# A hybrid SSD and GLA layer: the first block's gates one per step, and GpSimd's operand sums of the second part divided around the last head's power

## The chip, the cores and the metric

The kernel runs on one core of a Trainium2 chip. The metric is the time of one execution in microseconds (us), as the device measures it. The median of three runs of the kernel before is 2242.24 us.

A core has a tensor engine (TensorE, PE: matmuls from SBUF into PSUM banks), a vector engine (VectorE, DVE), a scalar engine (ScalarE, ACT: activation functions and copies), GpSimd (POOL) and a synchronisation engine (SyncE, SP), which here only issues transfers. Each engine works its own queue in order, and an instruction can wait for a semaphore that another engine or a DMA sets.

## The reference

One layer with two branches over the same input: `D_MODEL` is 1024, the sequence has 2048 tokens behind 16 learned meta tokens, all in float32. Cut to what matters here:

```python
u = rmsnorm(h, norm_w)
proj = u @ w_in                     # z, xbc, dt, q, k, v, g_gla, a_lr (rank 16), merge_g
xbc = silu(causal_depthwise_conv(xbc, conv_w, conv_b))            # 4 taps
y_ssd = ssd_chunked(xs, dt, a, bm, cm) + d_skip * xs              # 4 groups of 4 heads
y_ssd = group_rmsnorm(y_ssd * silu(z))
log_a = log_sigmoid(a_lr @ gla_gate_w2 + gla_gate_b) / 16         # 4 heads of 128
o = rmsnorm(gla_chunked(q, k, v, log_a))                          # 4 heads, chunks of 64
y_gla = o * silu(g_gla)
merged = sigmoid(merge_g[0]) * (y_ssd @ w_branch[0]) + sigmoid(merge_g[1]) * (y_gla @ w_branch[1])
out = rmsnorm(h + merged @ w_out)[meta:]
```

## The kernel before

**Numbers.** Every large matmul is an fp32 product made of three matmuls: each operand is divided into a high and a low part (`fp32r`), and `accum` (L214 to L216) adds high by high, high by low and low by high in PSUM. "Splitting" an operand means that ACT copies it into the high part and DVE subtracts the high part from the operand to get the low one.

**The first part** works through four blocks of 512 tokens (`nblk`; the first has the 16 meta tokens in addition, `m0`), up to about 1476 us. A block's work is a set of Python generators: the projections (`proj_zm`, `proj_conv`, `proj_z`, `proj_qk`, `proj_v`) one after another, and beside them the scans (`ssd_scan` for each of the four SSD groups, `gla_scan` for each of the four GLA heads) and the decay gates (`gates`). `step()` advances each running generator up to its next `yield`. So a `yield` says how far a generator's instructions come in one step, and what stands between them is a piece of a projection. The order of PE's and SP's queues is the order of the code (`tc.manual_schedule`); DVE, ACT and POOL are put in order by a scheduler that works with times of its own. `tc.issue_after(x)` tells that scheduler to place what follows behind instruction x; it adds no semaphore.

PSUM has eight banks in three pools: `pj` with three (projections, and in the first block the gates), `pt` with three (transposes) and `pc` with two (scans).

**The first block's gates.** `gates` makes the decay of the four heads in pairs. For each head h, PE multiplies with `gla_gate_w2` (L488, two matmuls of 264 columns in the first block, one into a bank of `pj` and one into a bank of `pt`); DVE (L490) and ACT (L491, absolute value) both read each bank. Behind the two heads of a pair ACT takes an exponential and a logarithm over both (L493, L494), and then a `yield` follows. In the first block the running sums of each head (L498 and one scan L500 for each chunk) are put off to the end of a step (`put_off`). At the same time the first block runs the convolution: PE's projection, eviction by ACT into two tiles (L595, L596), three multiply-adds on DVE (L600), tanh on ACT (L603), one more on DVE (L604), and then the first SSD group's scan: per chunk `before` (PE transposes L664, DVE, the decay mask with its square L680) and `after` (PE L689, L690 and L692, DVE).

**The last block's last head.** `gla_scan` ends with a norm: ACT sums squares, `rstd_of` scales on DVE (L258) and takes the power -0.5 on POOL (L259), ACT scales the four chunks (L969), PE transposes them (L976), DVE multiplies (L977) and ACT stores them (L980).

**The second part** does merge gates, branch products and the output product in stages. Each pair of output tiles is made of seven products in place of eight (products 1, 2, 6, 7, 5, 3, 4 in this order, `PS`). A product needs four B tiles (`load_b`, `prep_b`: ACT L1108, DVE L1109) and one A operand (`prep_a`: ACT L1133, DVE L1134), twelve matmuls for each operand. There are two operands n for each product at a time. `load_a` (L1115) loads four raw tiles `ar` of an operand; `sum_a` makes on POOL what the products need of them:

```python
nc.gpsimd.tensor_tensor(s1, a21, a22, op=ALU.add)         # L1124, product 5
nc.gpsimd.tensor_tensor(s2, s1, a11, op=ALU.subtract)     # L1125, product 6
nc.gpsimd.tensor_tensor(a21, a11, a21, op=ALU.subtract)   # L1126, product 7
nc.gpsimd.tensor_tensor(s4, a12, s2, op=ALU.subtract)     # L1127, product 3
```

The three sums go to tiles `as` (a ring of six, used by snapshots of PSUM as well), `a21` stays in place. The table `between` runs the second part's first loads, sums, splits and products (1, 2 and 6 of operands 0 and 1) in between the last steps of the last head; behind it, `at(pos, fn)` files an action for a position in the list of products and `run(i)` runs what is due.

## Time and the profile before

| | before |
|---|---|
| median of three runs | 2242.24 us (2240.61, 2242.24, 2245.01) |
| the profiled execution | 2246.45 us, its span 2244.7 us |
| PE matmul busy | 2211.9 us (99%), 11789 instructions |
| PE weight load busy | 1896.8 us (85%) |
| DVE busy | 1577.0 us (70%) |
| ACT busy | 1187.0 us (53%) |
| POOL busy | 693.9 us (31%) |
| DMA | 517.95 MB, mean 231 GB/s |
| granted PE clock, mean | 0.997 |

The busy times are of the profiled execution. Weight loads run beside matmuls, and the ends of matmuls are modelled, so 99% says that there is hardly a place where PE stands still, and not that it runs at its peak. Rows of a timeline give start and duration in us, engine, line, operation, output and inputs, tile shape, count, and in brackets the wait ahead of the instruction with what ended it. A group's row gives total busy time in us and the mean of one in ns. In the rows by stretch the engines stand in the order PE, weight loads, DVE, ACT, POOL, then the granted clock, the DMA share and GB/s. Names are those of the program without their numbers: `act`, `sq`, `c` and `tok4` are working tiles, `pj`, `pt` and `pc` PSUM banks, `whl` and `ue` the split weights and inputs of the first part, `a` and `b` the split operands of the second, `ar` and `br` their raw tiles.

### The profile page before, as it was taken

Reading aid. Unit: us, or ns where it says so; the run is one execution under the profiler, and the core shown is the slowest. Engines: PE = TensorE matmul, PEld = TensorE weight load, DVE = VectorE, ACT = ScalarE, POOL = GpSimd, SP = SyncE. Lnnn points to the kernel's source line nnn. Section 1 sums busy time; section 2 is a strip of 40 time slices with the busy share of each in tenths; the row PEclk is TensorE's granted clock in tenths of the full one; section 3 lists DMA queues with packets and bytes.
Section 4 is the critical chain, followed back from the end, with each engine's and each line's share of the span. In section 5 each row is a group of like instructions: output and inputs, shape, how many; then the busy total and the mean of one; then the engine's idle time right before and its main releaser. Section 6 shows DMA issues by size and latency. Waiting matters only on the chain.

```text
span 2244.7 us, 34971 instructions
## 1 busy us (share of the span) xinstructions
PE 2211.9 (99%) x11789; PEld 1896.8 (85%) x11789; DVE 1577.0 (70%) x2935; ACT 1187.0 (53%) x2767; POOL 693.9 (31%) x689
## 2 busy tenths in 40 slices
PE   7999999999999999999999999999999999999998
PEld 7999999888888888888988888878888888888887
DVE  5775676677557676567677666674679945789866
ACT  5666655575445456544465544454644545454544
POOL 5444433223212122221212100066233374324341
PEclk9999999999999999999999999999999999999999
DMA  9767875767777667778667664376768866787753
GB/s 313 247 222 234 273 259 202 237 209 240 240 244 260 212 213 237 241 245 272 207 212 233 213 211 160 127 250 198 241 227 289 303 221 217 237 282 245 261 177 121
DMA packets 313699, 517.95 MB, mean 231 GB/s; under 512 B 28080, under 2 KB 162480, under 8 KB 313520
## 3 DMA queue, kind: packets, MB, share of 16 engines
q1 hardware_dynamic: 247008, 419.89, 57.8%
q10 hardware_dynamic: 65872, 93.74, 11.5%
q8 instruction: 92, 1.51, 0.3%
q0 software_dynamic: 640, 2.10, 0.2%
q14 instruction: 87, 0.71, 0.1%
HBM read 368.42 MB, written 147.19 MB: 230 GB/s over the span
## 4 chain that ended last, share of the span: by engine, by line
PE 89%; DVE 4%; DMA 3%; ACT 2%; issue 1%; POOL 1%; SPq 0%; POOLq 0%; ACTq 0%; DVEq 0%
PE pj L214 20%; PE pj L216 20%; PE pj L215 19%; PE pt L215 4%; PE pt L214 4%; PE pt L216 4%; PE pc L689 2%; PE pc L214 2%; PE pc L216 2%; PE pc L215 2%; PE pc L850 2%; PE pc L690 1%; DMA acc<-in_xmt 1%; PE pc L692 1%; PE pc L958 1%
## 5 line engine op out<-in xcount | busy, mean ns | idle before, releaser
L214 PE MATMUL pj<-ue,whl 128*128 128x264 f32 (+1 forms) x672 | 235.3, 350 | 1.9 <-ACT acc L596 1.2
L216 PE MATMUL pj<-ue,whl 128*128 128x264 f32 (+1 forms) x672 | 229.7, 342 | 0.0
L215 PE MATMUL pj<-ue,whl 128*128 128x264 f32 (+1 forms) x672 | 228.8, 340 | 0.0
L214 PE MATMUL pj<-uo,whl 128*128 128x512 f32 x512 | 205.7, 402 | 0.0
L216 PE MATMUL pj<-uo,whl 128*128 128x512 f32 x512 | 200.1, 391 | 0.0
L215 PE MATMUL pj<-uo,whl 128*128 128x512 f32 x512 | 199.5, 390 | 0.0
L214 PE MATMUL pj<-b,a 128*128 128x512 f32 (+1 forms) x484 | 188.9, 391 | 0.7 <-DVE io L1252 0.5
L216 PE MATMUL pj<-b,a 128*128 128x512 f32 (+1 forms) x484 | 188.9, 390 | 0.3 <-DVE a L1134 0.3
L215 PE MATMUL pj<-b,a 128*128 128x512 f32 (+1 forms) x484 | 187.6, 388 | 0.0
L600 DVE SCALAR_TENSOR_TENSOR acc<-cin,hcw,acc 128x512 f32<-128x512 f32 (+1 forms) x192 | 156.7, 816 | 39.7 <-ACT acc L596 38.6
L83 POOL TENSOR_TENSOR wr<-wr 128x256 f32<-128x256 f32 x80 | 66.0, 826 | 371.8 <-DMA wr<-y 158.1
L1124 POOL TENSOR_TENSOR as<-ar,ar 128x512 f32<-128x512 f32 x40 | 62.9, 1572 | 374.7 <-DMA ar<-in_w_br 179.9
L1134 DVE TENSOR_TENSOR a<-ar,a 128x512 fp32r<-128x512 f32 x160 | 130.8, 824 | 65.0 <-ACT a L1133 63.5
L1109 DVE TENSOR_TENSOR b<-br,b 128x512 fp32r<-128x512 f32 x140 | 128.9, 943 | 18.1 <-ACT b L1108 17.8
L214 PEld LDWEIGHTS pj<-ue,whl 128*128 128x128 f32 x672 | 126.2, 188 | 17.7 <-ACT acc L596 1.7
L216 PEld LDWEIGHTS pj<-ue,whl 128*128 128x128 f32 x672 | 126.4, 188 | 14.9
L215 PEld LDWEIGHTS pj<-ue,whl 128*128 128x128 f32 x672 | 126.4, 188 | 14.7
L177 POOL TENSOR_TENSOR whl<-wr,whl 128x512 fp32r<-128x512 f32 (+1 forms) x76 | 96.9, 1282 | 126.2 <-ACT whl L175 94.4
L1168 ACT ACTIVATE sn<-pj 128x512 f32<-128x512 f32 x118 | 70.0, 593 | 123.8 <-PE pj L216 70.8
L1134 DVE TENSOR_TENSOR a<-as,a 128x512 fp32r<-128x512 f32 x120 | 101.6, 848 | 45.2 <-ACT a L1133 42.5
L1133 ACT ACTIVATE a<-ar 128x512 fp32r<-128x512 f32 x160 | 99.0, 624 | 64.7 <-PE pt L216 30.2
L215 PE MATMUL pt<-b,a 128*128 128x512 f32 x320 | 125.6, 392 | 3.9 <-DVE b L1109 3.9
(329 smaller groups left out, 6467.6 us busy)
## 6 DMA issues: line engine op xcount, KB each, us to landing
whl<-k_s SPq DMA_DIRECT2D x96, 512.0 KB, 3.7
whl<-k_g SPq DMA_DIRECT2D x96, 512.0 KB, 4.3
whl<-k_v SPq DMA_DIRECT2D x36, 512.0 KB, 4.0
wr<-in_w_feat SPq DMA_DIRECT2D x64, 256.0 KB, 4.5
k_s<-whl SPq DMA_DIRECT2D x32, 512.0 KB, 3.9
cb<-cumd SPq DMA_DIRECT2D x64, 256.0 KB, 5.1
y<-gg ACTq DMA_DIRECT2D x64, 256.0 KB, 4.2
k_g<-whl SPq DMA_DIRECT2D x32, 512.0 KB, 4.0
```

What stands on the lines that cost most here:

```text
L83: nc.gpsimd.tensor_tensor(o, x, y, op=ALU.subtract)
L177: nc.gpsimd.tensor_tensor(hl[:, 1], raw, hl[:, 0].bitcast(F32), op=ALU.subtract)
L214: nc.tensor.matmul(ps, sh, mh, start=first, stop=False, **kw)
L215: nc.tensor.matmul(ps, sh, ml, start=False, stop=False, **kw)
L216: nc.tensor.matmul(ps, sl, mh, start=False, stop=last, **kw)
L600: convd[:] = [nc.vector.scalar_tensor_tensor(acc, cin[:, k:k + tt], hcw[:, ti, k:k + 1], acc, op0=ALU.mult, op1=ALU.add)]
L689: nc.tensor.matmul(py[:, h * 64:(h + 1) * 64], dm[:, h], xdt[:, h], start=True, stop=True)
L1109: nc.vector.tensor_tensor(t[:, 1], raw, t[:, 0].bitcast(F32), op=ALU.subtract)
L1124: nc.gpsimd.tensor_tensor(s1, a21, a22, op=ALU.add)
L1133: nc.scalar.activation(t[:, 0], src, AF.Copy)
L1134: latest[:] = [nc.vector.tensor_tensor(t[:, 1], src, t[:, 0].bitcast(F32), op=ALU.subtract)]
L1168: nc.scalar.activation(sn, self.ps[n, "a"], AF.Copy)
```

## The change

**Gates.** In the first block `gates` now has a `yield` behind head 2. Head 3's matmuls, its evictions and the exponential and logarithm of the pair come one step later, and so does what the generator does behind them.

**Sums.** `sum_a` stays for later operands. For operands 0 and 1 of the second part it is divided: `sum_first` (s1 and s2) is called in row 2 of `between`, ahead of the last head's power; `sum_second` (the difference in `a21`) and `sum_third` (s4) are filed for positions -0.5 and 0. The last head's `rstd_of` is placed behind the last of the first sums, and the split of product 6 for operands 0 and 1 behind the last of the four scalings (L969), both with `issue_after`.

```diff
 # gates, inside the loop over the heads of a pair
                     evicted[:] = [nc.scalar.activation(g_all[:, h, a:a + n], ps[:, :n], AF.Abs, bias=gb)]
+                if m0 and h == 2:
+                    yield
             ga = g_all[:, h2:h2 + 2, :tt]
...
 # gla_scan, the norm at its end
-        r = rstd_of(ssq, 4, 1.0 / 256)
+        with tc.issue_after(summed[-1].ins) if o.b == nblk - 1 and h == GH - 1 and summed else nullcontext():
+            r = rstd_of(ssq, 4, 1.0 / 256)
         for c in range(NCH):
-            nc.scalar.activation(ot[:, c], ot[:, c], AF.Identity, scale=r[:, c:c + 1])
+            scaled[:] = [nc.scalar.activation(ot[:, c], ot[:, c], AF.Identity, scale=r[:, c:c + 1])]
...
-    early_b = {}
+    early_b, summed, scaled = {}, [], []
...
+        def sum_first(self, n):
+            a11, a21, a22, a12 = self.araws[n]
+            s1, s2 = [mk(rpl, [P, 4, P], F32, "as", bufs=NAS) for _ in range(2)]
+            nc.gpsimd.tensor_tensor(s1, a21, a22, op=ALU.add)
+            summed[:] = [nc.gpsimd.tensor_tensor(s2, s1, a11, op=ALU.subtract)]
+            self.a[n].update({4: a22, 5: s1, 6: s2})
+
+        def sum_second(self, n):
+            a11, a21, a22, a12 = self.araws[n]
+            nc.gpsimd.tensor_tensor(a21, a11, a21, op=ALU.subtract)
+            self.a[n][7] = a21
+
+        def sum_third(self, n, s2):
+            a12 = self.araws.pop(n)[3]
+            s4 = mk(rpl, [P, 4, P], F32, "as", bufs=NAS)
+            nc.gpsimd.tensor_tensor(s4, a12, s2, op=ALU.subtract)
+            self.a[n][3] = s4
...
         def prep_a(self, n, p):
...
-            nc.scalar.activation(t[:, 0], src, AF.Copy)
+            with tc.issue_after(scaled[-1].ins) if n < 2 and p == 6 and self is stages[0] else nullcontext():
+                nc.scalar.activation(t[:, 0], src, AF.Copy)
...
+    second = {}
+
+    def first_sums(n):
+        st.sum_first(n)
+        second[n] = st.a[n][6]
+
+    for n in range(2):
+        at(-0.5, lambda n=n: st.sum_second(n))
+        at(0, lambda n=n: st.sum_third(n, second[n]))
...
     between = {
...
-        2: [lambda: st.prep_a(0, 1), lambda: st.prep_a(1, 1)],
+        2: [lambda: st.prep_a(0, 1), lambda: st.prep_a(1, 1), lambda: first_sums(0), lambda: first_sums(1)],
         3: [lambda: early(0, 1), lambda: st.prep_a(0, 2)],
-        4: [lambda: st.sum_a(0), lambda: early(1, 1), lambda: st.prep_a(1, 2)],
+        4: [lambda: early(1, 1), lambda: st.prep_a(1, 2)],
         5: [lambda: early(0, 2), lambda: st.prep_b(6, 0), lambda: st.load_b(6, 2)],
-        6: [lambda: early(1, 2), lambda: st.sum_a(1), lambda: st.prep_b(6, 1), lambda: st.load_b(6, 3)],
+        6: [lambda: early(1, 2), lambda: st.prep_b(6, 1), lambda: st.load_b(6, 3)],
```

What this moves in the engines' queues is shown at three places. A row has line, operation, output and inputs, and shape; the lines of the kernel after the change are 2 higher behind `gates`, 3 higher behind the norm and 22 higher from `prep_a` on.

PE before, at the gates of heads 2 and 3 in the first block: `w` is the gate's weight, `c` and `sq` are operands of the first SSD group's scan, and `pj_1603` is the first bank of the second group's z projection.

```order
L488 MATMUL pj_1550<-act_1005,w_387 128x264
L488 MATMUL pt_1554<-act_1005,w_387 128x264
L488 MATMUL pj_1558<-act_1005,w_387 128x264
L488 MATMUL pt_1562<-act_1005,w_387 128x264
L664 MATMUL pt_1568<-cst,act_682 128x128
L664 MATMUL pt_1568<-cst,act_772 128x128
L664 MATMUL pt_1568<-cst,act_858 128x128
L689 MATMUL pc_1588<-c_179_1440,sq_1447 128x64 x4
L690 MATMUL pc_1588<-s_ssd,act_936 128x256
L692 MATMUL pc_1594<-c_180_1442,bt_1445 128x256
L214 MATMUL pj_1603<-whl_1605,ue_313 128x256
```

PE after, at the same place, with the z projection's first bank `pj_1593`, and then the place one step later (48 matmuls of that projection stand between them):

```order
L488 MATMUL pj_1550<-act_1005,w_387 128x264
L488 MATMUL pt_1554<-act_1005,w_387 128x264
L666 MATMUL pt_1558<-cst,act_682 128x128
L666 MATMUL pt_1558<-cst,act_772 128x128
...
L214 MATMUL pj_1593<-whl_1595,ue_313 128x256
...
L488 MATMUL pj_1655<-act_1005,w_387 128x264
L488 MATMUL pt_1659<-act_1005,w_387 128x264
L691 MATMUL pc_1667<-c_200_1562,sq_1569 128x64 x4
```

Head 3's two matmuls have moved from in front of the first chunk's transposes to in front of the next chunk's scan, behind half of the z projection.

POOL before, at the last head's power (`rstd_16657`; `rstd_16421` is the head before it) and the sums of operands 0 (`ar_16589` to `ar_16595`) and 1 (`ar_16597` to `ar_16603`):

```order
L259 TENSOR_TENSOR rstd_16421<-rstd_16421,mhalf 128x4
L259 TENSOR_TENSOR rstd_16657<-rstd_16657,mhalf 128x4
L1124 TENSOR_TENSOR as_16682<-ar_16591,ar_16593 128x512
L1125 TENSOR_TENSOR as_16683<-as_16682,ar_16589 128x512
L1126 TENSOR_TENSOR ar_16591<-ar_16589,ar_16591 128x512
L1127 TENSOR_TENSOR as_16684<-ar_16595,as_16683 128x512
L1124 TENSOR_TENSOR as_16758<-ar_16599,ar_16601 128x512
L1125 TENSOR_TENSOR as_16759<-as_16758,ar_16597 128x512
L1126 TENSOR_TENSOR ar_16599<-ar_16597,ar_16599 128x512
L1127 TENSOR_TENSOR as_16760<-ar_16603,as_16759 128x512
```

POOL after (the power is now `rstd_16665`):

```order
L259 TENSOR_TENSOR rstd_16421<-rstd_16421,mhalf 128x4
L1136 TENSOR_TENSOR as_16657<-ar_16591,ar_16593 128x512
L1137 TENSOR_TENSOR as_16658<-as_16657,ar_16589 128x512
L1142 TENSOR_TENSOR ar_16591<-ar_16589,ar_16591 128x512
L1136 TENSOR_TENSOR as_16661<-ar_16599,ar_16601 128x512
L1137 TENSOR_TENSOR as_16662<-as_16661,ar_16597 128x512
L259 TENSOR_TENSOR rstd_16665<-rstd_16665,mhalf 128x4
L1142 TENSOR_TENSOR ar_16599<-ar_16597,ar_16599 128x512
L1148 TENSOR_TENSOR as_16863<-ar_16595,as_16658 128x512
L1148 TENSOR_TENSOR as_16865<-ar_16603,as_16662 128x512
```

Five of the eight sums stand in front of the power, where none stood; three stay behind it.

DVE before, at the low parts of product 7's B tiles (`b_3077` to `b_3080`), among those of the A operands (`as_16682` and `as_16758` are s1, `as_16684` and `as_16760` are s4):

```order
L1134 TENSOR_TENSOR a_16861<-as_16682,a_16861 128x512
L1109 TENSOR_TENSOR b_3077_16843<-br_16835,b_3077_16843 128x512
L1134 TENSOR_TENSOR a_16864<-as_16758,a_16864 128x512
L1109 TENSOR_TENSOR b_3078_16846<-br_16837,b_3078_16846 128x512
L1134 TENSOR_TENSOR a_16867<-as_16684,a_16867 128x512
L1109 TENSOR_TENSOR b_3079_16849<-br_3075_16839,b_3079_16849 128x512
L1109 TENSOR_TENSOR b_3080_16852<-br_16841,b_3080_16852 128x512
L1134 TENSOR_TENSOR a_16911<-as_16760,a_16911 128x512
```

DVE after, where the same four are `b_3075` to `b_3078`, `as_16661` is s1 of operand 1, and `as_16863` and `as_16865` are s4:

```order
L1156 TENSOR_TENSOR a_16860<-as_16661,a_16860 128x512
L1112 TENSOR_TENSOR b_3075_16837<-br_16829,b_3075_16837 128x512
L1112 TENSOR_TENSOR b_3076_16840<-br_16831,b_3076_16840 128x512
L1112 TENSOR_TENSOR b_3077_16843<-br_3073_16833,b_3077_16843 128x512
L1112 TENSOR_TENSOR b_3078_16846<-br_16835,b_3078_16846 128x512
L1156 TENSOR_TENSOR a_16867<-as_16863,a_16867 128x512
L1156 TENSOR_TENSOR a_16911<-as_16865,a_16911 128x512
```

The splits of product 5's operand 1 and of product 3's operand 0 have left the gaps between the four.

## The prediction

> **What bounds the kernel now.** I read the page first, then the list of what TensorE (PE) waited for, and then the timeline at the two places where the change moves instructions.
>
> ```profile
> PE 2211.9 (99%) x11789; PEld 1896.8 (85%) x11789; DVE 1577.0 (70%) x2935; ACT 1187.0 (53%) x2767; POOL 693.9 (31%) x689
> PE 89%; DVE 4%; DMA 3%; ACT 2%; issue 1%; POOL 1%; SPq 0%; POOLq 0%; ACTq 0%; DVEq 0%
> ```
>
> PE is busy for 99% of the span and carries 89% of the chain that ended last. So nothing that other engines save counts unless PE waited for it. The list of PE's waits over the whole run (total us, times, longest) is short, and two of its lines are the two places of the change:
>
> ```profile
> PE pt L215 <- DVE b L1109: 3.9, 3, 1.7
> PE pj L488 <- ACT acc L596: 3.1, 1, 3.1
> PE pj L216 <- DVE a L1134: 0.3, 1, 0.3
> ```
>
> The second line is the first block's gates; the other two lie at the start of the second part. Together they are 7.3 us, 0.33% of the run. A measurement of this kernel can tell about 0.2%, 4.5 us, from no change.
>
> **The first part of the change: one gate a step.** PE's timeline there, and the granted clock by stretch (the number in front of the DMA share):
>
> ```profile
> 104.16 0.28 PE L488 MATMUL pt<-act,w 48*128 48x264 f32 x1
> 107.58 0.58 PE L488 MATMUL pj<-act,w 48*128 48x264 f32 x1 [3.15 <-ACT acc L596]
> 108.32 0.90 PE L664 MATMUL pt<-cst,act 128*128 128x128 f32 x3
> 109.01 1.80 PE L689 MATMUL pc<-c,sq 128*128 128x64 f32 x8
> 112.07 0.78 PE L214 MATMUL pj<-whl,ue 128*128 128x256 f32 x1
> 113.58 0.28 PE L214 MATMUL pj<-whl,ue 128*128 128x256 f32 x1
> 118.56 1.00 PE L689 MATMUL pc<-c,sq 128*128 128x64 f32 x8
> 120.12 0.47 PE L214 MATMUL pj<-whl,ue 128*128 128x256 f32 x1
> ```
>
> ```profile
> 106.50:113.40 6.90, 5.82 (x22) 5.23 (x23) 6.72 (x14) 6.90 (x19) 4.09 (x4) 0.51 0.51 169
> 113.40:120.00 6.60, 6.60 (x56) 6.55 (x55) 5.76 (x12) 5.46 (x10) 1.25 (x1) 1.00 0.21 64
> ```
>
> The matmul of gate h=3 waits 3.15 us for ACT's eviction of the convolution's PSUM bank. PE has three banks in pool pj: two hold the convolution, the third took gate h=2, so gate h=3 needs the first one back. That eviction stands behind L603 on ACT, which waits for VectorE (DVE):
>
> ```profile
> 105.54 0.64 ACT L603 ACTIVATE act<-acc 128x528 f32<-128x528 f32 x1 [2.17 <-DVE acc L600]
> 106.97 0.56 ACT L596 ACTIVATE acc<-pj,hcb,hcw 128x264 f32<-128x264 f32 x1
> 98.23 2.93 DVE L500 TENSOR_TENSOR_SCAN g_all<-ones_r,tok 128x16 f32<-128x16 f32 x5
> 105.76 0.68 DVE L680 TENSOR_TENSOR sq<-sq,sq 128x512 f32<-128x512 f32 x1
> ```
>
> The wait costs twice. After it the clock is at 0.51 for 6.9 us, so what follows is slow: L689 to L692 took 109.01 to 112.07, 3.06 us, where the same work took 118.56 to 120.12, 1.56 us, a step later. From 107.58 to 118.56 PE needed 10.98 us. At the full clock the same work is two gate matmuls (0.5), three transposes (0.4, by the eight of 1.04 us below), 1.56, and 48 matmuls of the z projection, of which the last 42 took 118.56 - 113.58 = 4.98, so 48 take 5.7: 8.2 us in all. The slow clock cost 2.8, the whole wait 3.15 + 2.8 = 5.95 us.
>
> With the change PE goes from gate h=2 straight to L664 and L689. L664 needs a bank of pt and features that are long done, so it ends at about 104.85. L689 then needs L680 on DVE, whose queue up to there is unchanged and which ends at 105.76 + 0.68 = 106.44: a new wait of 1.6 us. PE's L689 to L692 end at about 108.0, and the z projection takes the convolution's two banks, which ACT has let go at 107.5 and, one more pair of such instructions later, at about 108.3 (the second is needed 24 matmuls after the first). So it runs without a wait to 113.7; then come gate h=3, whose bank (that of h=2) was read by DVE and ACT right behind 108.3, and the next L689 at about 114.1, where it was 118.56. **Gain 5.95 - 1.6 = 4.35 us.** The lower bound is a new wait that slows the clock as well: 1.55 us. The upper bound is no new wait: 5.95 us. I take 4.35, because three waits at the second place show what 1.7 us does to the clock:
>
> ```profile
> 1477.16 0.50 PE L215 MATMUL pt<-b,a 128*128 128x512 f32 x1 [0.46 <-DVE b L1109]
> 1480.54 0.50 PE L215 MATMUL pt<-b,a 128*128 128x512 f32 x1 [1.73 <-DVE b L1109]
> 1483.90 0.50 PE L215 MATMUL pt<-b,a 128*128 128x512 f32 x1 [1.71 <-DVE b L1109]
> 1476.00:1486.00 10.00, 6.11 (x25) 4.09 (x24) 10.00 (x9) 5.14 (x10) 7.04 (x5) 1.00 0.57 181
> ```
>
> It stays at 1.00. The Trainium skill, "TensorE: Matmul & The Clock Gate" (Why this matters for your kernels), says that idle gaps of more than about 3 us bring half the clock; the trace agrees on both sides, 0.51 after 3.15 us and 1.00 after 1.73 us, and by that rule too the new wait of 1.6 us would be harmless.
>
> What moves besides: gate h=3's two evictions on DVE and ACT, and ScalarE's exponential and logarithm for both gates, come a projection piece later, and so do the two running sums (L498 and five scans L500, about 3.1 us each on DVE). The first now stands where the second stood, the second behind the next convolution's L600. DVE has room there; these are its idle times in the trace of before, and ACT's next eviction waits for PE, not PE for it:
>
> ```profile
> 131.18 0.69 DVE L680 TENSOR_TENSOR sq<-sq,sq 128x512 f32<-128x512 f32 x1 [1.99 <-ACT sq L679]
> 141.42 0.42 DVE L667 TENSOR_TENSOR c<-pt,tkd 128x256 f32<-128x256 f32 x1 [1.86 <-PE pt L664]
> 140.73 0.39 ACT L595 ACTIVATE cin<-pj 128x264 f32<-128x264 f32 x1 [1.29 <-PE pj L216]
> ```
>
> So 3.1 - 1.86 = 1.2 us of DVE's work runs into the next step, whose eviction has 1.3 us to spare. I cost it at nothing; without that cover PE would wait by what is over. The queue of SyncE (SP) keeps its order in the whole program, so no load is overtaken.
>
> **The second part: sums in front of the last power.** In the trace of before GpSimd (POOL) does the last head's power and then sums, four for each of three operands. These are the power, the first sum and the last of the third operand:
>
> ```profile
> 1460.98 1.01 POOL L259 TENSOR_TENSOR rstd<-rstd,mhalf 128x4 f32<-128x4 f32 x1 [13.67 <-DVE rstd L258]
> 1461.96 1.30 POOL L1124 TENSOR_TENSOR as<-ar,ar 128x512 f32<-128x512 f32 x1
> 1481.60 1.71 POOL L1127 TENSOR_TENSOR as<-ar,as 128x512 f32<-128x512 f32 x1
> ```
>
> While POOL sums, DVE's splits of the operands are slow. DVE's groups in the stretch with sums and in the one after it, with the mean in ns behind the busy time:
>
> ```profile
> L1109 DVE TENSOR_TENSOR b<-br,b 128x512 fp32r<-128x512 f32 x4 | 5.9, 1490 | 0.0
> L1109 DVE TENSOR_TENSOR b<-br,b 128x512 fp32r<-128x512 f32 x8 | 5.0, 678 | 0.0
> ```
>
> The same split takes 1490 ns beside sums and 678 ns without. One split even waited for its sum, through ACT, and PE began the seventh product before its operands were split:
>
> ```profile
> 1472.48 1.10 DVE L1134 TENSOR_TENSOR a<-as,a 128x512 fp32r<-128x512 f32 x1 [1.25 <-ACT a L1133]
> 1476.08 0.62 PE L214 MATMUL pt<-b,a 128*128 128x512 f32 x2
> ```
>
> So PE waited 0.46 + 1.73 + 1.71 = 3.9 us at L1109's results, and 0.3 us before that.
>
> Five of the first eight sums now stand in front of the power, the rest behind it. When can they run? The third and the seventh of the eight loads decide (issue times in the first row of each pair, us to landing in the second):
>
> ```profile
> L1115 SPq DMA_DIRECT2D ar<-in_w_feat x1: 328/328/328, 1450.8 to 1450.8; - x1
> DMA to landing us min/median/max: 3.3/3.3/3.3
> L1115 SPq DMA_DIRECT2D ar<-in_w_feat x2: 430/430/430, 1452.1 to 1452.6; - x2
> DMA to landing us min/median/max: 6.0/6.0/6.1
> ```
>
> They land at 1454.1 and 1458.7. Three sums of 1.3 run from 1454.1 to 1458.0, two more from 1458.7 to 1461.3, or to 1462.0 where DVE's splits of the first products (at 1458.2 to 1459.5) get in their way. So the power starts 0.3 to 1.0 us later than at 1460.98. Behind it wait ACT's four scalings and PE's eight transposes, in a fixed order:
>
> ```profile
> 1452.18 1.04 PE L976 MATMUL pt<-cst,ot 128*128 128x128 f32 x8
> 1462.05 1.70 ACT L969 ACTIVATE ot<-ot,rstd 128x256 f32<-128x256 f32 x4
> 1463.28 1.29 PE L976 MATMUL pt<-cst,ot 128*128 128x128 f32 x8
> ```
>
> The last head's transposes took 1.29 us against 1.04 for the eight of the head before it, so they already wait for the scalings. ACT now also has one split in front of them (0.5). PE loses about 0.8 us here.
>
> What it gains: fewer sums lie beside the splits from 1462 on, the wait of 1.25 us for a sum goes, and in the new order all four L1109 of the seventh product stand in front of the third product's splits. Behind the power's DVE instruction there are nineteen of about 0.68 us to the last of these four, 12.9 us; from 1461.2 on, with 2.4 for waits and the three sums that remain, DVE is through at 1476.5. PE reaches the seventh product at about 1476.3 and wants the last of the four some 4 us later. So 3.9 + 0.3 = 4.2 us of waits go.
>
> Not all of it stays. The seventh product is 24 matmuls, 0.23 us apart by the row at 1476.08 (0.62 less one matmul of 0.39), 5.5 us, so PE reaches the fifth product at 1481.8. The third operand's sums still fall on about 1476 to 1483. At 1.5 us a split, DVE makes two for the third product and then the fifth's four, done at 1481.0, 1482.5, 1484.0 and, behind the sums, 1484.7. PE wants them at 1482.0, 1482.7, 1483.4 and 1484.1: late by 0.6, and I add 0.2 for loads. **Gain 4.2 - 0.8 - 0.8 = 2.6 us.** Bounds: 0 if late loads and splits take all of it, 4.2 if nothing is late. Behind that PE's demand is 2.8 us for four splits of 0.68 (an operand's twelve matmuls) and then the same splits again for the second operand, so DVE draws ahead again.
>
> **The sum.** 4.35 + 2.6 = 6.95 us. The profiled execution took 2246.45 us (span 2244.7), 4.2 above the median of the runs, 2242.24. Taken from the median: 2242.24 - 6.95 = **2235.3 us**.
>
> **The rivals.** First, the gates pay and the second place does not: the power is late by more and the operands' loads limit PE. For it speaks that the loads land when they land, and SP's order is the same. 2242.24 - 4.35 = 2237.9 us.
>
> Beside this: the Trainium skill, "SBUF — State Buffer" (SBUF: two separate sides), speaks against the change. It says that GpSimd and a VectorE operation with two inputs in SBUF exclude each other for the whole instruction; 1490 against 678 ns agrees. What it makes of this change, from rows: five sums of 1.3 us in front of the power meet four splits of 0.68; if each split holds up a sum, the power is 4 x 0.68 = 2.7 us late, and all of the second gain is gone. This is the same 2237.9 us. I hold it for less likely, since only three of the four splits lie in that time and loads, not POOL, end the first three sums.
>
> Second, the timed runs of before do not all drop the clock at the gates. The wait of 3.15 us then costs only itself, and the first gain is 3.15 - 1.6 = 1.55: 2242.24 - 1.55 - 2.6 = 2238.1 us. For it speaks the spread of the three runs, 2240.61 to 2245.01.
>
> Third, the gates' wait only changes its place, because L689 or the z projection waits as long as gate h=3 did: 2242.24 - 2.6 = 2239.6 us. Against it speaks that DVE's L680 ends at 106.44.
>
> Fourth, slower: the two running sums, now in neighbouring steps, hold up DVE's L600 of the second group's convolutions, so that ACT's L603 and the eviction behind it come late, as at 105.54. That is the place and the mechanism of the wait just removed, at 5.95 us each. It decides from 1.3 us of delay at the eviction on. Two such waits give 2 x 5.95 - 6.95 = +4.95, 2247.2 us. For it speaks that the removed wait itself came a step after such a pair (the scans at 98.23); against it, DVE's idle 1.99 and 1.86 us.
>
> **How the numbers follow.** The forecast has 0.60, the first rival 0.14, the second 0.10, the third 0.07, the fourth 0.07, and 0.02 is left for no effect at all. The bound of 0.2% lies at 2237.8. The forecast lies beyond it except for its outer edge, and of the first and second rivals, which lie on the bound, I count four tenths as faster: 0.57 + 0.10 = 0.67 faster. Slower are the fourth rival and a little beside it, 0.09; the rest, 0.24, is the same. The low end is both upper bounds, 5.95 + 4.2 = 10.15: 2232 us. The high end takes in the third rival: 2240 us.
>
> **What would show it.** Right: PE's list of waits has no L488 line of 3 us, a new one at L689 for DVE's L680 of 1 to 2 us stands near 106.5, the granted clock between 106.5 and 113.5 is near 1.00, and the next L689 starts near 114. At the second place POOL's power starts between 1456.5 and 1458 (4.35 us earlier by the first gain, up to 1 later by the sums), and the waits for L1109 sum to less than 1.5 us. Wrong: the clock is at 0.5 again after the new wait, PE waits for the scalings by over 2 us, the waits at L1109 stay near 3.9, or new waits for L596 stand between 125 and 160.

## The result and the profile after

The change takes 2237.82 us in the median of 11 runs (2233.59 to 2240.65), the kernel before 2242.24 us on the same chip: 4.4 us less, a ratio of 0.9979 with a 95% interval of 0.9972 to 0.9987, or 2.9 to 6.3 us. The profiled execution of the change took 2236.02 us, 1.8 below its median; that of before was 4.2 above its own. So the two traces lie 10.4 us apart where the medians lie 4.4 apart, and a difference of the traces may not be read as the gain.

The lines of the changed kernel are 2 to 22 higher than before: L689 is L691, L680 is L682, L1109 is L1112, L976 is L979, L969 is L972. The list of PE's waits after the change (total us, times, longest), cut to what answers to the three lines shown of before:

```profile
PE pc L691 <- DVE sq L682: 1.6, 1, 1.6
PE pt L979 <- ACT ot L972: 0.3, 1, 0.3
```

The 3.1 us at gate 3 and the 3.9 + 0.3 us at the second part's splits are gone; in their place stand 1.6 us at the first scan and 0.3 us at the last head's transposes. PE's timeline at the gates, and the granted clock by stretch (the number in front of the DMA share):

```profile
102.12 0.39 PE L488 MATMUL pj<-act,w 48*128 48x264 f32 x1
104.66 1.77 PE L691 MATMUL pc<-c,sq 128*128 128x64 f32 x8 [1.56 <-DVE sq L682]
107.69 0.77 PE L214 MATMUL pj<-whl,ue 128*128 128x256 f32 x1
114.39 1.10 PE L691 MATMUL pc<-c,sq 128*128 128x64 f32 x8
```

```profile
101.49:104.90 3.41, 1.85 (x13) 1.33 (x12) 3.41 (x9) 1.24 (x5) 0.00 (x0) 1.00 0.75 257
104.91:108.32 3.41, 3.41 (x14) 3.05 (x14) 3.41 (x8) 3.41 (x11) 3.01 (x4) 0.50 0.12 41
108.32:114.00 5.68, 5.68 (x49) 5.55 (x48) 4.88 (x10) 2.99 (x9) 1.08 (x2) 1.00 0.80 251
```

The new wait is the forecast one, 1.56 us. But the clock falls to 0.50 behind it, for 3.41 us, and the scan that follows takes 3.03 us (104.66 to 107.69) where the prediction's rows have 1.56 at the full clock. The prediction had named a clock of 0.5 behind the new wait as a sign that it is wrong.

At the second place, DVE and POOL around the last head's power:

```profile
1454.14 1.20 DVE L258 TENSOR_SCALAR rstd<-ssq 128x4 f32<-128x4 f32 x1
```

```profile
1453.68 1.63 POOL L1137 TENSOR_TENSOR as<-as,ar 128x512 f32<-128x512 f32 x1
1455.43 1.39 POOL L259 TENSOR_TENSOR rstd<-rstd,mhalf 128x4 f32<-128x4 f32 x1
```

```profile
1457.41 1.97 PE L979 MATMUL pt<-cst,ot 128*128 128x128 f32 x8 [0.31 <-ACT ot L972]
```

The fifth sum (L1137) ends at 1455.31, the power begins 0.12 us later, and PE's eight transposes take 1.97 us where they took 1.29. Behind that no matmul of product 7 waits. The power begins ahead of the forecast window of 1456.5 to 1458, because this execution is also earlier where the code is the same; its place in the stretch is compared further below.

To compare traces whose starts and other waits differ, I use two stretches of PE's queue that hold the same matmuls in every kernel. Stretch A runs from the start of gate 2's first matmul to the start of the 150th behind it, stretch B from the twelfth matmul in front of the last head's transposes over 137 matmuls, both by the start times in each trace. The rows by stretch give their length behind the window: before (A, then B), then the change (A, then B):

```profile
103.93:128.64 24.71, 21.56 (x152) 20.60 (x151) 20.70 (x43) 17.68 (x40) 9.89 (x9) 0.86 0.49 162
1460.51:1497.14 36.63, 32.19 (x138) 24.65 (x137) 33.11 (x37) 25.10 (x49) 24.87 (x17) 1.00 0.73 242
```

```profile
102.12:124.61 22.49, 20.93 (x151) 19.77 (x151) 16.87 (x37) 17.81 (x41) 9.41 (x9) 0.92 0.59 189
1454.16:1486.59 32.43, 31.68 (x139) 24.99 (x138) 30.02 (x37) 23.56 (x45) 18.06 (x12) 1.00 0.78 258
```

In this pair the gates are worth 2.2 us and the second part 4.2. The rest of the difference of the traces, some 4 us, lies where the code is the same.

All runs, with both stretches; the column "before" has the median of the kernel before on the same chip. Behind the first two rows come three groups of four kernels, one chip for each group. The medians are of 10 or 11 runs, those of the two kernels without the sum of head 1 of 9 and 5:

| kernel | median us | before | ratio (95% interval) | A, us | B, us |
|---|---|---|---|---|---|
| before | 2242.24 | | | 24.71 | 36.63 |
| the change | 2237.82 | 2242.24 | 0.9979 (0.9972 to 0.9987) | 22.49 | 32.43 |
| gates alone | 2238.85 | 2242.35 | 0.9986 (0.9977 to 0.9995) | 20.87 | 34.34 |
| sums alone | 2239.78 | 2242.35 | 0.9990 (0.9981 to 0.9998) | 24.88 | 32.83 |
| power first | 2240.53 | 2242.35 | 0.9992 (0.9983 to 1.0001) | 20.81 | 35.87 |
| sum of head 1 one step later | 2238.04 | 2242.35 | 0.9978 (0.9969 to 0.9987) | 20.35 | 32.59 |
| the change again | 2238.22 | 2242.43 | 0.9983 (0.9974 to 0.9992) | 20.85 | 32.98 |
| four sums | 2238.38 | 2242.43 | 0.9981 (0.9972 to 0.9990) | 20.81 | 31.87 |
| sum of head 1 behind gate 3 | 2237.54 | 2242.43 | 0.9980 (0.9971 to 0.9989) | 19.02 | 33.32 |
| behind gate 3, and four sums | 2238.29 | 2242.43 | 0.9983 (0.9974 to 0.9992) | 19.02 | 32.40 |
| before, no sum of head 1 | 2236.86 | 2242.61 | 0.9977 (0.9967 to 0.9987) | 19.03 | 35.70 |
| the change, no sum of head 1 | 2235.32 | 2242.61 | 0.9967 (0.9954 to 0.9979) | 19.02 | 32.77 |
| sum of head 1 with gate 3 | 2238.18 | 2242.61 | 0.9981 (0.9972 to 0.9990) | 21.22 | 35.00 |
| the same, four sums | 2237.67 | 2242.61 | 0.9977 (0.9968 to 0.9985) | 21.21 | 32.73 |

An interval is some 4 us wide, so the medians tell a gain of 4 us from none, and hardly one of 1 us.

### The profile page after: what moved, and what is told of

Same layout as the page of the kernel before. It is cut to its first block, busy times and chain, and to the rows that moved or that the text cites. A ratio compares the mean times of both kernels' runs of the same rounds, so it can differ in the third digit from the quotient of the medians.

```text
span 2233.9 us, 34963 instructions
## 1 busy us (share of the span) xinstructions
PE 2209.5 (99%) x11789; PEld 1896.3 (85%) x11789; DVE 1575.5 (71%) x2935; ACT 1187.8 (53%) x2767; POOL 690.4 (31%) x689
## 4 chain that ended last, share of the span: by engine, by line
PE 90%; DMA 4%; DVE 3%; ACT 1%; issue 1%; SPq 0%; POOL 0%; POOLq 0%; ACTq 0%; DVEq 0%
PE pj L214 20%; PE pj L216 20%; PE pj L215 20%; PE pt L214 4%; PE pt L215 4%; PE pt L216 4%; PE pc L691 2%; PE pc L214 2%; PE pc L216 2%; PE pc L215 2%; DMA acc<-in_xmt 2%; PE pc L852 2%; PE pc L692 1%; PE pc L694 1%; PE pc L960 1%
## 5 line engine op out<-in xcount | busy, mean ns | idle before, releaser
L1127 POOL TENSOR_TENSOR as<-ar,ar 128x512 f32<-128x512 f32 x38 | 57.0, 1500 | 377.1 <-DMA ar<-in_w_br 147.5
L1112 DVE TENSOR_TENSOR b<-br,b 128x512 fp32r<-128x512 f32 x140 | 126.6, 930 | 14.7 <-ACT b L1111 13.9
```

What stands on the lines that cost most here:

```text
L1112: nc.vector.tensor_tensor(t[:, 1], raw, t[:, 0].bitcast(F32), op=ALU.subtract)
```

## The experiments

**Each edit alone.** The gates' `yield` in the kernel before; and the change without it:

```diff
 # gates alone: the kernel before, and
+                if m0 and h == 2:
+                    yield
```

> The kernel before with the yield behind gate 2 alone; the second part's sums as they were. In the trace of after, PE waits 1.56 us for DVE's square of the decay mask where it waited 3.15 us for a bank, and the clock is at 0.50 for 3.41 us where it was for 6.83; from the first gate to the next chunk's scan the stretch is 2.4 us shorter. Theory 1 (both edits pay): 2242.24 - 2.4 = 2239.8 us, and in this trace the same wait of 1.5 to 1.7 us; the clock drops behind it or not, by where the wait falls in the clock's grid of 3.41 us. Theory 2 (the gates pay as forecast and the sums do nothing in most runs): 2237.9 us. Theory 3 (the gates' wait only changed its place): 2242 us.

```diff
 # sums alone: the change, less the yield
-                if m0 and h == 2:
-                    yield
```

> The change without the yield: only the second part's sums are divided. In the trace of after, PE's waits for product 7's splits are gone (4.18 us and about 1.1 us of restarts) and PE loses 1.0 us at the last head's transposes. Theory 1 (both edits pay): 2242.24 less 2 to 4.4, 2237.8 to 2240.2 us, and a trace without waits at product 7, with the 3.1 us wait at gate 3 as before. Theory 2 (only the gates pay): 2242 us. Theory 3 (only the sums pay): 2237.8 us.

Measured: 2238.85 us, 3.5 less than before, and 2239.78 us, 2.6 less. Theory 1 holds: both edits pay; neither interval holds 1. It is the second run that decides, since 2238.85 lies as far from theory 1's 2239.8 as from theory 2's 2237.9. PE's wait and the clock in the trace of the gates alone:

```profile
105.46 1.10 PE L691 MATMUL pc<-c,sq 128*128 128x64 f32 x8 [1.59 <-DVE sq L682]
```

```profile
100.83:104.24 3.41, 3.04 (x23) 2.52 (x21) 3.41 (x8) 0.96 (x4) 0.00 (x0) 1.00 0.91 290
104.24:107.65 3.41, 2.19 (x15) 2.09 (x16) 3.41 (x9) 3.15 (x9) 1.79 (x2) 1.00 0.03 11
```

The wait is the same, 1.59 us, and here the clock stays up. In every trace the clock changes only at points of a grid of 3.41 us (the low stretches inside the runs last 3.41 or 6.83 us), which lies differently against the program in each execution. In the change's trace the whole wait fell in one step of the grid (101.49 to 104.90), here it is spread over two. So stretch A is 20.87 us here and 22.49 there with the same queue order on PE. That a wait lies whole in one step isn't enough, though: the last section has such steps after which the clock stayed up.

**The power first.** The change with all eight sums behind the power:

```diff
-        with tc.issue_after(summed[-1].ins) if ... else nullcontext():
-            r = rstd_of(ssq, 4, 1.0 / 256)
+        r = rstd_of(ssq, 4, 1.0 / 256)
...
-        2: [..., lambda: first_sums(0), lambda: first_sums(1)],
+        4: [lambda: first_sums(0), ...],
+        6: [..., lambda: first_sums(1), ...],
```

> The change with the last head's power in front of all eight sums again; the order of the sums themselves (first two sums and the difference of each operand, then the two last sums) and the yield stay as in the change. If it is the sums' place in front of the power that pays, five sums of 1.3 to 1.6 us lie beside the splits again, PE waits 2 to 4 us at product 7's splits, and the time is 2240 to 2242 us. If it is that the last sums are late and product 7's splits stand in front of product 3's, there is no wait of over 0.5 us at product 7, the 1.0 us at the last head's transposes is gained back, and the time is about 2236.8 us, 1.0 less than the change.

Measured: 2240.53 us, 1.7 more than the gates alone on the same chip, so the new order of the sums without their new place brings nothing that the runs can tell. PE's waits in that trace:

```profile
1468.47 0.50 PE L215 MATMUL pt<-b,a 128*128 128x512 f32 x1 [1.04 <-DVE b L1111]
1477.52 0.50 PE L215 MATMUL pj<-b,a 128*128 128x512 f32 x1 [2.31 <-DVE b L1111]
```

Stretch B is 35.87 us, as without the edit, and the splits of the B tiles are slow again. DVE's groups from the power on, here and in the change:

```profile
L1111 DVE TENSOR_TENSOR b<-br,b 128x512 fp32r<-128x512 f32 x9 | 13.4, 1518 | 0.7 <-ACT b L1110 0.7
L1112 DVE TENSOR_TENSOR b<-br,b 128x512 fp32r<-128x512 f32 x10 | 9.4, 983 | 0.2 <-ACT b L1111 0.2
```

The first branch holds by the traces: what pays is that five sums are over before the splits of the B tiles begin. (The medians alone don't show it: 1.7 us is less than an interval.) The second wait is at product 5 and not, as expected, at product 7: the late splits are passed on from one product to the next.

**Four sums in front of the power.** The fifth is placed behind the scalings with `issue_after`; in POOL's queue it then stands right behind the power:

```diff
-            nc.gpsimd.tensor_tensor(s1, a21, a22, op=ALU.add)
-            summed[:] = [nc.gpsimd.tensor_tensor(s2, s1, a11, op=ALU.subtract)]
+            summed[:] = [nc.gpsimd.tensor_tensor(s1, a21, a22, op=ALU.add)]
             self.a[n].update({4: a22, 5: s1, 6: s2})
+            if n == 0:
+                nc.gpsimd.tensor_tensor(s2, s1, a11, op=ALU.subtract)
+
+        def sum_behind(self, n):
+            with tc.issue_after(scaled[-1].ins):
+                nc.gpsimd.tensor_tensor(self.a[n][6], self.a[n][5], self.araws[n][0], op=ALU.subtract)
...
-        3: [lambda: early(0, 1), lambda: st.prep_a(0, 2)],
+        3: [lambda: st.sum_behind(1), lambda: early(0, 1), lambda: st.prep_a(0, 2)],
```

> The change with the fifth of the sums in front of the power (the second sum of operand 1) placed behind the last head's scalings; four stay in front. In the trace of the change DVE's scaling of 128x4 numbers in front of the power took 1202 ns beside that fifth sum and ended 0.03 us behind it, where its median is 170 ns, and the power took 1.39 us beside DVE's split, where it takes 1.01. Theory 1 (an instruction of DVE with operands in SBUF waits for the end of POOL's): without the fifth sum the scaling takes 0.2 us, the power begins within 0.4 us of the last sum of squares (1.4 us before), PE's eight transposes take 1.0 to 1.3 us in place of 1.97, and the time is 1.0 us less than the change's on the same chip. Theory 2 (the four sums and DVE's splits are late all the same, or the fifth sum now holds up product 6): the transposes stay at 1.9 us or PE waits for product 6, and the time is that of the change or up to 1 us above it.

DVE and PE in that trace:

```profile
1453.50 0.16 DVE L258 TENSOR_SCALAR rstd<-ssq 128x4 f32<-128x4 f32 x1
```

```profile
1456.36 1.47 PE L979 MATMUL pt<-cst,ot 128*128 128x128 f32 x8
```

The same instruction on 512 numbers takes 0.16 us without a sum beside it and took 1.20 beside one; the transposes take 1.47 us in place of 1.97, without a wait in front. That is theory 1's direction, at 0.8 us by the rows (0.5 and the wait of 0.31), where 1.0 was expected and transposes of 1.0 to 1.3. Stretch B is 31.87 us, the shortest of all. The median, 2238.38 us against 2238.22 for the change, doesn't show it: 0.8 us is less than these runs resolve.

The run doesn't tell whether the fifth sum held up the power through DVE's scaling or simply by standing in front of it in POOL's queue, for both are gone. A trace of a later kernel, with five sums in front and the sum of head 1 in the step of gate 3, does:

```profile
1453.71 1.08 DVE L258 TENSOR_SCALAR rstd<-ssq 128x4 f32<-128x4 f32 x1
1454.83 1.70 POOL L1142 TENSOR_TENSOR as<-as,ar 128x512 f32<-128x512 f32 x1
1456.50 1.46 POOL L259 TENSOR_TENSOR rstd<-rstd,mhalf 128x4 f32<-128x4 f32 x1
```

DVE's scaling is done at 1454.79 here, and the power still begins only when the fifth sum ends, at 1456.50. So the queue is enough; the slow scaling adds nothing here, and in the change at most the 0.12 us between the end of the sum and the power.

**Where the backlog goes.** Five kernels put off the first block's running sum of head 1, which loads DVE just ahead of the two waits. One step later, the change otherwise:

```diff
+                if m0 and h == 1:
+                    yield
                 if m0:
                     put_off.append(sums)
                 else:
                     sums()
-                yield
-            if m0 and not h2:
                 yield
```

> The change, and in the first block the running sum of head 1 (one subtraction and five scans, about 5 us from 94.4 to 99.3 us with what lies between) is put off by one more step, so that DVE has it behind the square that PE waits for. If DVE's backlog from these scans is the cause of the old wait at gate 3 and of the new one at the scan, both are gone: no PE wait of over 0.3 us between 100 and 116 us, the clock stays at 1.00 there, 1.56 + 1.7 = 3.2 us less than the change, about 2234.6 us. If the backlog only moves on, a wait of 1 to 3 us stands one step later (at a bank that the convolution's eviction holds, or at the next scan), and the time is that of the change, 2237.8 us.

Behind gate 3, in front of head 2's sum (`held_sum` keeps it until then):

```diff
+        held_sum = []
...
-                def sums(h=h):
+                def sums(h=h, gmt=gmt):
...
-                if m0:
+                if m0 and h == 1:
+                    held_sum.append(sums)
+                elif m0:
+                    if held_sum:
+                        put_off.append(held_sum.pop())
+                        yield
                     put_off.append(sums)
```

> The change, and in the first block the running sum of head 1 is put off behind gate 3, in front of that of head 2, so that each of the three later sums stands in a step of its own with DVE's idle time in front of it. If the backlog that these scans leave on DVE makes the wait at the first group's scans and DVE has room for them later, no PE wait of over 0.3 us stands between 100 and 116 us nor in the 25 us behind it, the clock stays at 1.00, and the time is 1.6 us less than the change's in runs where the clock didn't drop and 3.2 less where it did, 2.0 to 2.8 in the median. If the backlog moves on as with one step, a wait of 1 to 3 us stands at 120 to 140 us, and the time is that of the change.

The same with four sums in front of the power:

> Both edits, the sum of head 1 behind gate 3 and four sums in front of the power. If both theories hold, about 3 us less than the change, 2234.8 us; if only one does, 1 or 2 us less; if neither, the time of the change.

In the step of gate 3 itself (`held_sum` and `sums` as above):

```diff
             nc.scalar.activation(ga, ga, AF.Ln, bias=1.0)
+            if held_sum:
+                put_off.append(held_sum.pop())
             yield
...
-                if m0:
+                if m0 and h == 1:
+                    held_sum.append(sums)
+                elif m0:
                     put_off.append(sums)
```

> The change, and the first block's running sum of head 1 is put off to the step of gate 3, a piece of the z projection in which DVE has no convolution's multiply-adds to do, one step ahead of the sum of head 2. If it is room on DVE that counts, neither the wait at 104 us nor one at 112 us (as with one step) nor one at 151 us (as behind gate 3, three sums in neighbouring steps) is there, and the time is 1.6 to 3 us less than the change's 2238.2. If three sums in a row are too many wherever they stand, a wait of 1 to 2 us stands between 120 and 150 us, and the time is that of the change.

And this with four sums in front of the power:

> The kernel with the sum of head 1 in the step of gate 3, and four sums in front of the last head's power (the fifth behind the scalings). In the traces the fifth sum's place was worth 0.9 us at the transposes (1.96 against 1.47 us, and a wait of 0.46 less), in the medians nothing that the runs could tell. If both count, 2.5 to 4 us less than the change, about 2235 us; if only the transposes do, 1 us less.

Beside them ran the change once more:

> The change itself once more, beside the three that follow. If the gates' part depends on where the wait falls in the clock's grid of 3.41 us (the wait of 1.56 us dropped the clock in the trace of the change and the same wait did not in two other traces), this trace has the wait of 1.5 to 1.6 us at the scan again, and the clock at 0.50 behind it only if nearly all of the wait lies in one step of the grid. The time is 2237 to 2239 us.

Measured: 2238.04, 2237.54, 2238.29, 2238.18 and 2237.67 us, none of them told apart from the change's 2237.82 and 2238.22. PE's timeline says why. One row each from the kernel with the sum one step later, behind gate 3, and with gate 3:

```profile
112.36 1.08 PE L691 MATMUL pc<-c,sq 128*128 128x64 f32 x8 [1.30 <-DVE sq L682]
```

```profile
152.75 0.66 PE L697 MATMUL pc<-c,sq 128*128 128x64 f32 x4 [1.54 <-DVE sq L688]
```

```profile
121.91 0.39 PE L214 MATMUL pj<-ue,whl 128*128 128x264 f32 x1 [1.95 <-DVE tok L524]
```

Wherever the sum is put, a wait of 1.3 to 1.95 us stands behind it or behind the two sums that follow it. The wait at 104 us is gone each time, and stretch A goes down to 19.02 us where the new wait lies behind it, but the time is back at 112, 122 or 152 us. The rival expectation held with the sum one step later and in the step of gate 3; behind gate 3 it held too, but for the place (152 us, not 120 to 140). The four sums beside it brought nothing that the medians show. In the second trace of the change itself the wait is 1.57 us, about half of it in each of two steps of the grid, and the clock stays up, as expected.

With the sum in the step of gate 3 the way to PE is another one. DVE stood idle in front of L524, and what it waited for was ACT:

```profile
114.57 0.48 ACT L492 ACTIVATE g_all<-pj,pv 128x264 f32<-128x264 f32 x1 [3.95 <-DVE tok L491]
121.16 0.69 DVE L524 SCALAR_TENSOR_TENSOR tok<-tok,pj 128x512 f32<-128x512 f32 x1 [4.19 <-ACT tok L523]
```

DVE's scans held up the evictions of gate 3 (L491), ACT waited 3.95 us for them, and behind its own evictions ACT had the pair's exponential and logarithm and two table loads of 1.28 us each before L523.

**What the waits cost.** In the kernel before and in the change, head 1's running sum is left out:

```diff
-                if m0:
+                if m0 and h == 1:
+                    pass
+                elif m0:
                     put_off.append(sums)
```

> The kernel before, with the first block's running sum of head 1 (a subtraction and five scans, 3.6 us of DVE) left out, and so that part of the computation. DVE then has no backlog at 95 to 105 us, and the wait of 3.15 us at gate 3 should be gone with its slow clock. The difference to the kernel before is what that wait costs in the timed runs, on average. By the prediction's sum 5.95 us (3.15 and 2.8 of slow clock): 2236.4 us. If the clock stays up in most timed runs, 3.15 us: 2239.2 us. If another wait takes its place, under 2 us: 2240.5 us or more.

> The change with the same running sum of head 1 left out. PE's wait of 1.5 to 1.6 us at the scan should be gone. The difference to the change (2238.2 us in its second measurement) is what the new wait costs on average: 1.6 us if the clock stays up behind it in most timed runs (2236.6 us), 3.1 us if it drops in most (2235.1 us). The difference to the kernel before without the sum is the second part's gain alone, 2.0 to 4.4 us.

Stretch A of the kernel before without that sum:

```profile
101.90:120.93 19.03, 18.88 (x152) 18.27 (x152) 18.04 (x35) 16.09 (x38) 9.27 (x9) 1.00 0.60 192
```

Here PE waits for nothing and the clock is at 1.00. So the old wait cost 24.71 - 19.03 = 5.7 us in the trace, and 2242.61 - 2236.86 = 5.75 us in the medians: the timed runs pay for the slow clock too. The new wait costs 20.85 - 19.03 = 1.8 us where the clock stays up and 22.49 - 19.03 = 3.5 us where it falls; in the medians 2238.22 - 2235.32 = 2.9 us, between two chips, or 7.3 - 4.2 = 3.1 us if each is taken against the kernel before on its own chip. That lies nearer to the second.

The timed runs have no timeline, but the mean granted clock of each is on record, and it says more on how often the clock falls than the traces do (in one of five with this wait). In the 14 runs of the two kernels without the sum it is 0.9991 in the mean, and 0.999 or above in each. In the 33 runs of the change, of its second measurement and of the kernel with four sums, which have the same order at the gates, it is 0.9985 in the mean. It is 0.998 in 17 of them, which take 2239.1 us in the mean, where the other 16 take 2237.0. In 90 runs of the kernel before it is 0.9979. Half clock for a share of a run lowers its mean clock by half of that share, so over some 2236 us the difference of 0.0006 is about 2.7 us at half clock in an average run, where one step of the grid is 3.41; the difference of 0.0012 is 5.4 us, where the trace of before has 6.83. So the clock seems to fall in most timed runs, behind the old wait and behind the new one.

## Why the prediction was right, and where its terms were off

The forecast was 2235.3 us with a range of 2232 to 2240; 2237.82 lies in it, and the change is faster, as forecast. Of the forecast gain of 6.95 us, 4.4 came.

- **What bounds, and the old wait's price.** Right. Leaving the cause out took 5.75 us off the median, where the step had 5.95. The interval, 2.9 to 7.4 us, would still hold the second rival, by which the timed runs of before don't drop the clock and the wait costs its 3.15 us only. The recorded clock of those runs speaks against it: 0.9979 in the mean, 5.4 us at half clock.
- **The new wait.** Its place, engine and size were right: L689's successor for DVE's square, 1.56 us where 1.6 was forecast, in all five traces with this order at 1.53 to 1.59. Its price was mis-sized. The step that failed is "it stays at 1.00", taken from three waits at the second place: the clock fell in the change's own trace. By the traces the first term is 24.8 - 20.85 = 4.0 us (24.8 is the mean of stretch A in the two traces with the old wait) or 24.8 - 22.49 = 2.3, by the medians 5.75 - 2.9 = 2.9; I had 4.35 and kept the slow clock only as the lower bound of 1.55. By the recorded clocks the fall is the rule and not the exception.
- **The z projection and the neighbouring sums.** Right: no new wait for the convolution's eviction stands between 105 and 160 us, so the slower rival did not come. A relative of its mechanism is real, though. The five kernels that moved head 1's sum each had a wait behind the scans, at 1.3 to 1.95 us and not at 5.95; but PE waited for the scan's square or for L524 and not, as the rival has it, for the convolution's eviction.
- **The second part's sum.** The size was right, and in part by luck, since terms that were off made up for each other. Stretch B is 36.63, 34.34 and 35.70 us in the three traces with the old sums, 35.6 in the mean, and 32.43, 32.83, 32.98, 32.59, 33.32, 32.77 and 35.00 in the seven with the new ones and all five sums in front, 33.1: 2.4 us, where 2.6 was forecast. In the medians the sums alone brought 2.6 us, and 1.5 in the pair without head 1's sum (2236.86 - 2235.32). The wait that I had taken from the trace of before was its largest; others had less to remove.
- **The power.** "0.3 to 1.0 us later" was right in size and in cause. Before, the power began 0.47 us behind the stretch's start (1460.51 and 1460.98), after it 1.27 us (1454.16 and 1455.43): 0.8 later, because the fifth sum stands in front of it in POOL's queue. PE lost 1.0 us at the transposes (0.31 and 1.97 - 1.29), where 0.8 was forecast. What the prediction overlooked is the small DVE instruction in front of the power, which stood still for the fifth sum, 1.20 us where it takes 0.16 with four sums. The Trainium skill, "SBUF — State Buffer" (SBUF: two separate sides), has a rule that fits it, an exclusive lock for the whole instruction; the trace agrees, since L258 ends at 1455.34, 0.03 us behind the sum. The prediction used the rule for a rival on the sums alone. It cost nothing to speak of here, as the power had to wait for that sum in its own queue.
- **The late splits of product 5.** The 0.8 us was about right where it came (matmuls of product 5 that start 0.3 to 1.1 us late in sum, in five of the ten traces with the new sums) and nothing in the change's own trace.

The first rival, the gates alone at 2237.9 us, gives the measured median almost exactly, and yet it isn't what happened: the sums alone are faster than before on their own. Both edits pay, the first less than forecast. By the traces they should bring 2.3 + 2.4 = 4.7 to 4.0 + 2.4 = 6.4 us together; the two measurements of the change have 4.4 and 4.2, with intervals up to 6.3 and 5.8. The lower end fits best, which is again what a clock that mostly falls would give. The 0.3 to 0.5 us that remain are less than the runs' scatter.

## What to carry to other kernels

In this kernel a wait of the bounding engine that came from another engine's backlog moved when the order changed, and went only when work left the busy stretch: four places of one running sum gave one time within 1 us, and leaving it out gave 3 to 6. Price a stall of the tensor engine with the clock that may follow it. For the clock take the worst case that a trace shows, not the one beside it, and look at the mean clock of the timed runs, since one trace is one draw. And before a sum is put on GpSimd in front of something on the critical chain, look at what stands behind it in GpSimd's own queue, and at the VectorE instructions beside it: even a scaling of 128x4 numbers waited here for the end of a sum.

## What the hardware showed that was not expected

The clock falls after waits far under 3.41 us, and the share of time in which PE is busy doesn't decide it. The two steps of the clock's grid around the moved wait, first in the kernel with the sum behind gate 3, then in the one that has four sums as well:

```profile
150.61:154.02 3.41, 1.87 (x16) 1.61 (x15) 3.41 (x9) 2.22 (x7) 0.89 (x1) 1.00 0.53 185
154.03:157.44 3.41, 3.41 (x15) 3.15 (x14) 3.41 (x8) 3.26 (x11) 2.70 (x4) 0.50 0.43 142
```

```profile
149.79:153.20 3.41, 1.87 (x17) 1.64 (x15) 3.41 (x9) 1.24 (x4) 0.00 (x0) 1.00 0.66 216
153.20:156.61 3.41, 3.41 (x26) 3.31 (x27) 3.41 (x8) 3.41 (x12) 2.85 (x3) 1.00 0.17 60
```

PE is busy for 1.87 of 3.41 us in both, with the same wait of 1.54 us inside, and the next step is at 0.50 in one and at 1.00 in the other. The work differs: in the second most of it is projection, in the first it is mostly transposes and the scan's small matmuls. In the change's own trace (1.85 us, and the clock fell) the step has some of each. But that isn't the rule as it stands either. In the kernel with the sum in the step of gate 3 most of the wait of 1.95 us lies in a step whose work is eight small matmuls of the next group's scan, transposes and three projection matmuls. PE is busy for less of it, and the clock stays up:

```profile
118.23:121.64 3.41, 1.73 (x16) 1.51 (x14) 0.48 (x1) 3.38 (x5) 0.00 (x0) 1.00 0.13 49
121.65:125.06 3.41, 3.15 (x26) 3.16 (x27) 2.97 (x8) 3.41 (x11) 3.23 (x3) 1.00 0.39 141
```

In the same kernel the clock fell at the second part:

```profile
1456.25:1459.66 3.41, 1.95 (x8) 0.87 (x6) 1.44 (x2) 1.67 (x5) 2.95 (x3) 1.00 0.39 134
1459.67:1463.08 3.41, 3.34 (x12) 2.84 (x12) 2.81 (x5) 3.41 (x8) 0.00 (x0) 0.50 0.70 201
```

There a wait of 1.32 us for the scalings and slow transposes fill the end of the step. The Trainium skill, "TensorE: Matmul & The Clock Gate" (Part 1: The HAM clock gate), speaks of a free-running window of 3413 ns, and the traces agree with its length; that an idle window is needed for the clock to fall doesn't agree, since these were more than half busy. Which measure of the work decides is open; no run here tried it.
